# A hybrid decoder layer in emulated fp32: spread sums at the change of x, channel-major norms, and z loads placed earlier in the steps without Strassen

## The chip, the core and the metric

The kernel runs on one core of one Trainium2 chip. The metric is the device time of one execution in microseconds. Before the change it is 1374.56 us, the median of three runs (1373.44 to 1375.09).

## What is computed

One decoder layer over 2048 tokens of width 1024, all in fp32. The reference, cut to its core:

```python
def reference(x, ln_g, w_in, conv_w, lru_conv_w, ..., w_out, final_g):
    xn = rms_norm(x, ln_g)                                   # 2048 x 1024
    b_gate, c_gate, x_conv, g_conv, x_lru, g_lru = split(xn @ w_in)   # w_in: 1024 x 6144
    y_conv = b_gate * causal_conv3(c_gate * x_conv)          # 8 heads of 128 channels
    y_conv = headwise_rms_norm(y_conv, 8, conv_out_g) * silu(g_conv)
    y_lru = rg_lru_mixer(x_lru, ...)    # causal conv of width 4, two sigmoid gates per
                                        # token, scan over tokens; 16 heads of 64 channels
    y_lru = headwise_rms_norm(y_lru, 16, lru_out_g) * silu(g_lru)
    y = concatenate([y_conv, y_lru])                         # 2048 x 2048
    return rms_norm(x + y @ w_out, final_g)                  # w_out: 2048 x 1024
```

## The kernel before

**Products.** TensorE multiplies in a reduced format, so each fp32 operand is cut into a high part and a remainder. `mm` (L910) issues, for each product of blocks, sh·th, sh·tl and sl·th. The stationary side S is the weights (or z in the output projection), the moving side T is x (or w_out). Each block product of the projections is one level of a Strassen scheme: seven products per *step*, numbered 0 to 6. A product takes one *slot* of 12 matmuls of 128x512. Sums of products are formed on the way out: ScalarE copies a partial bank to `q1` after product 0 (L1220), to `u2` after product 1 (L1223) and to `rr` after product 2 (L1226), and VectorE adds these to other banks. Products 0, 1 and 2 accumulate in the same bank A, so product 1 waits for the copy to q1 and product 2 for the copy to u2.

**Steps.** The list `steps` has 48 steps of the input projection (`l`, `a`, `b` are its three kinds: the LRU group and its gate, the convolution's c and x, the convolution's b and gate), first for token half h=0 (from here on: half 0), then for half 1, and 16 steps `o` of the output projection, in two phases of eight (m = 0..7, 256 tokens each). T stays on chip as tiles `th`/`tl` within such a set of steps. There are three set changes: x of half 0 to x of half 1 (about 545 to 590 us), x to w_out for phase 0 (about 1020 to 1070 us), and the other half of w_out's rows for phase 1 (about 1195 to 1250 us).

**Set changes.** The step ahead of a change is *new*, the one behind it *opens* the set and is computed *plainly*, that is with eight block products and no Strassen, since the sums of T do not exist yet; the next is *late*. Class `Change` (L412) has a call `slot(q)` for every slot from the new step (q = 0 to 7) over the plain step (8 to 15) to the late step (16 to 21). It loads pieces of T, forms the sums (x: `sums`, four subtractions on VectorE for each of four j, at q = 9 to 12; w_out: the sums were made long before and stand in DRAM as `td`) and cuts pieces (`cut`: ScalarE casts th, VectorE subtracts to get tl). The late step takes its products in the order `AFTER` (L220) instead of `ORDER`.

**Order of the work.** Everything is under a manual schedule: program order is the order on each engine, and each engine works in that order. SP issues nearly all DMAs, also in that order, and an issue that waits for a buffer or for data holds all later ones. `at(n, f)` puts f n slots ahead; `tick()` at the head of each slot runs what is due. `load_next` (L932) loads the stationary operand for the step after next: for the input projection raw weights or cut tiles kept in DRAM (`sd`), for the output projection z. `load_z` (L269) loads y from `yd` into four `raw` pieces, the reciprocal norms from `rsd`, broadcast over partitions, into `zr`, and VectorE multiplies them (`raw<-raw,zr`). Pieces `raw` and `traw` share a pool of eight buffers, taken in turn.

**Consumers.** Each `l` step feeds `lru` (L653): a convolution, cutting u into `st` on VectorE, gate matmuls on PE (`gates`), sigmoids, a scan; `finish` (L608) multiplies the gain and the SiLU gate into `gl` (or `gb` for the convolution group), stores it to `yd`, squares y and calls `head_sums` (L598), one VectorE instruction that transposes 32x32 blocks and sums 32 tokens in each (`sums<-r`, `sums<-t`, 1024 elements per partition). After all 16 head groups of a half `head_norms` (L559) cuts the sums into `rt`, adds over channels on PE (`norm_ps`), takes the root on ScalarE and the reciprocal on VectorE (`hn`), and stores 24 pieces to `rsd` (L587). `gl`, `gb` and the residual rows `xr` take turns in two buffers of the tag `o2`. `outp` adds the residual: `xr<-xr,ob` in phase 0, `ob<-ob,xr` in phase 1, where xr comes by DMA.

The functions that the diff touches, with the line numbers of the profile:

Of the kernel before, what the change touches and what calls it, by code (L numbers as in the profile page):

```python
# [12 lines left out]
F32 = mybir.dt.float32  # L13
# [25 lines left out]
def hymba_kernel(ctx: ExitStack, tc: tile.TileContext, x, xt, w_in, par, lamc, w_gate, w_out, final_g, out):  # L39
# [14 lines left out]
    rsd = [dram.tile([2, NB, 3 * KT, P], F32, name=f"rsd{h}") for h in range(2)]  # L54
# [165 lines left out]
    AFTER = (0, 4, 5, 1, 3, 2, 6)  # L220
# [48 lines left out]
    def load_z(h, m, zr, wait):  # L269
        r = [piece("raw") for _ in range(4)]  # L270
        fs = []
        for i in range(2):
            c, b = divmod(2 * m + i, NB)
            assert normed[c // 2]
            rs_ = rsd[c // 2][c % 2]
            zz_, zq_ = [], []
            z2 = wt(("u", "r")[i], "zr") if zr else None
            for q in range(2):
                zz = r[2 * i + q].rearrange("p (k t) -> p k t", k=NB)
                zq = z2[:, q * C:(q + 1) * C] if zr else piece("zr")  # L280
                k0 = (1 - h) * KT + q * NB
                nc.sync.dma_start(zz, yd[c][b, :, k0:k0 + NB, :])
                zq = zq.rearrange("p (k t) -> p k t", k=NB)
                if h == 1:
                    nc.sync.dma_start(zq, rs_[b:b + 1, k0:k0 + NB, :].broadcast_to((P, NB, P)))
                else:
                    nc.sync.dma_start(zq[:64], rs_[b:b + 1, k0:k0 + NB, :].broadcast_to((64, NB, P)))
                    k0 += KT
                    nc.sync.dma_start(zq[64:], rs_[b:b + 1, k0:k0 + NB, :].broadcast_to((64, NB, P)))
                fs.append(lambda zz=zz, zq=zq: tt(zz, zz, zq, ALU.mult))  # L290
# [121 lines left out]
    class Change:  # L412
        def __init__(self, t, dst):
# [4 lines left out]
            self.order = [(i, j) for i in (5, 4, 0, 7, 1, 2, 3, 6) for j in range(NB)]  # L418
# [22 lines left out]
        def sums(self, j):  # L441
            b11, b12, b21, b22 = (self.r[i, j] for i in (0, 7, 4, 5))
            tt(b11, b12, b11, ALU.subtract)
            tt(b12, b22, b12, ALU.subtract)
            tt(b22, b22, b11, ALU.subtract)
            tt(b21, b21, b22, ALU.subtract)
            for i, v in ((2, b11), (3, b12), (1, b22), (6, b21)):
                self.r[i, j] = v

        def of_x(self, q):  # L450
# [11 lines left out]
            if 9 <= q <= 12:  # L462
                self.sums(q - 9)
            self.cut({1: ((5, 0), (5, 1)), 2: ((5, 2), (5, 3)), 4: ((0, 0), (0, 1)), 5: ((4, 0), (4, 1)),
# [3 lines left out]
                      18: ((6, 0),), 19: ((6, 1),), 20: ((6, 2),), 21: ((6, 3),)}.get(q, ()))  # L468
# [90 lines left out]
    def head_norms(h):  # L559
# [17 lines left out]
        def root():  # L577
            v["rs"] = aux("hn")[:NR, 0:KT * R]
            nc.scalar.activation(out=v["rs"], in_=v["ps"], func=AF.Sqrt, scale=inv_hd, bias=eps[:NR])

        def store():
            for w in range(3):
                k0 = (w + 1) % 3 * KT
                for i in range(2):
                    for b in range(NB):
                        p0 = w * R + (i * NB + b) * 4
                        nc.sync.dma_start(  # L587
                            rsd[h][i, b, k0:k0 + KT, :].rearrange("k (q r) -> q k r", q=4),
                            v["rs"][p0:p0 + 4].rearrange("q (k r) -> q k r", k=KT))
# [8 lines left out]
    def head_sums(h, kt, y):  # L598
        if summed[0] == 0:
            sums[0] = psn.tile([P, 2 * KT * R], F32, tag="sums", name="sums")  # L600
        nc.vector.tensor_reduce(out=sums[0][:, kt * R:(kt + 1) * R], in_=y.rearrange("p (a r) -> p r a", r=R),
# [6 lines left out]
    def finish(d0, h, kt, y, sil, gain):  # L608
# [10 lines left out]
        at(d0 + (1 if kt == KT and h == 0 else 2), store)  # L619
# [334 lines left out]
    with tc.manual_schedule(engines={ENG.PE, ENG.Activation, ENG.DVE, ENG.Pool, ENG.SP}):  # L954
# [182 lines left out]
        for n in range(PLAIN, N):  # L1137
# [5 lines left out]
            put = lru(h, k, 2) if opens(n) and kind == "l" else consumer[kind](h, k)  # L1143
            if n == 3 * KT + 6:
                work_on[0] = jobs()
            if opens(n):
                cc = {}
                for s, (which, i, t) in enumerate(((12, 1, 5), (22, 3, 5), (11, 1, 4), (21, 3, 4),
# [12 lines left out]
                    if s == 5:  # L1161
                        load_next(n + 2, 3)
# [123 lines left out]
```

## Time and profile before

| | |
|---|---|
| median of the runs (lowest to highest) | 1374.56 us (1373.44 to 1375.09) |
| the profiled execution's own time | 1373.37 us |
| its span | 1371.5 us |
| PE matmul busy | 1304.3 us, 95% |
| DVE (VectorE) busy | 1054.6 us, 77% |
| ACT (ScalarE) busy | 746.6 us, 54% |
| POOL (GpSimd) busy | 226.2 us, 16% |
| DMA | 355.29 MB, mean 259 GB/s |

PE's share says that the span is PE's work plus about 67 us in which it waited. In a row of a timeline the first two numbers are the start and the length in us, and a bracket at the end gives how long the engine idled just before and what released it. A group's row (page, part 5) gives busy time, mean ns of one, and the idle time before its instructions. The granted clock of TensorE is a column of its own in the table by stretches. L163 is the helper that issues every two-operand VectorE instruction and L915 the line of every projection matmul, so these rows are told apart by the names of their tiles.

### The profile page before, as it was taken

The page shows a single profiled execution, that of the slowest core. Times are in us where ns is not written, and L with a number is a line of the kernel's source. Part 1 is how long each engine was busy: PE and PEld are TensorE (multiplying, and loading weights), DVE is VectorE, ACT ScalarE, POOL GpSimd, SP SyncE. Part 2 cuts the span into 40 slices and gives each one's busy share as a digit, 9 for nine tenths or more (in the row PEclk, how much of TensorE's full clock was granted, in tenths as well). Part 3 has the DMA queues.
Part 4 walks back from the last instruction along what each step waited for, and adds up shares of the span by engine and source line. Part 5 has one row for each costly group of instructions (what it writes and reads, how often), then busy time and mean ns, then how long its engine had stood idle before and what let it go on. Part 6 is the DMA issues. An engine that isn't in the chain of part 4 may idle for free.

```text
span 1371.5 us, 16702 instructions
## 1 busy us (share of the span) xinstructions
PE 1304.3 (95%) x5648; PEld 1059.7 (77%) x5648; DVE 1054.6 (77%) x1243; ACT 746.6 (54%) x1138; POOL 226.2 (16%) x160
## 2 busy tenths in 40 slices
PE   6979999999999999898999999999999889998997
PEld 5867777787878787786888888888877678887886
DVE  6778897898989888967566785776557767659885
ACT  7475658566575667564554636364465323444443
POOL 2203333243334331101010110101100000000000
PEclk9999999999999999999999999999999999999999
DMA  7137797988989887551799999999788697797743
GB/s 282 31 127 257 279 262 264 283 318 272 344 287 321 286 289 258 172 171 50 260 318 293 330 357 317 321 361 344 232 272 282 199 253 232 244 397 270 240 149 135
DMA packets 162454, 355.29 MB, mean 259 GB/s; under 512 B 18496, under 2 KB 53312, under 8 KB 162368
## 3 DMA queue, kind: packets, MB, share of 16 engines
q1 hardware_dynamic: 162080, 353.90, 76.1%
q8 instruction: 45, 0.74, 0.2%
q14 instruction: 41, 0.34, 0.1%
q10 hardware_dynamic: 288, 0.32, 0.1%
HBM read 217.11 MB, written 137.04 MB: 258 GB/s over the span
## 4 chain that ended last, share of the span: by engine, by line
PE 39%; DMA 6%; DVE 4%; ACT 3%; issue 1%; SPq 0%; DVEq 0%; ACTq 0%
PE bank L915 38%; DMA traw<-td 3%; DMA zr<-rsd 2%; DVE tl L163 1%; PE gate L695 1%; ACT i L702 1%; ACT r L702 1%; DVE s L163 1%; DMA od<-xr 1%; DMA xr<-in_x_dram 0%; DVE raw L163 0%; ACT q L1220 0%; DVE ob L163 0%; ACT th L427 0%; DMA raw<-yd 0%
## 5 line engine op out<-in xcount | busy, mean ns | idle before, releaser
L915 PE MATMUL bank<-th,s 128*128 128x512 f32 x3632 | 1141.1, 393 | 32.7 <-ACT q L1220 15.1
L915 PEld LDWEIGHTS bank<-th,s 128*128 128x128 f32 x3632 | 686.8, 189 | 188.0 <-ACT u L1223 19.3
L915 PE MATMUL bank<-tl,s 128*128 128x512 f32 x1816 | 711.4, 392 | 1.2 <-DVE tl L163 0.9
L915 PEld LDWEIGHTS bank<-tl,s 128*128 128x128 f32 x1816 | 343.7, 189 | 74.0 <-DVE tl L163 2.5
L163 POOL TENSOR_TENSOR s<-raw,s 128x512 fp32r<-128x512 f32 x62 | 109.5, 1778 | 250.1 <-ACT s L200 209.7
L200 ACT CAST s<-raw 128x512 fp32r<-128x512 f32 x140 | 84.5, 616 | 67.6 <-PE bank L915 44.8
L163 DVE TENSOR_TENSOR tl<-traw,th 128x512 fp32r<-128x512 f32 x117 | 83.3, 747 | 40.7 <-ACT th L427 30.3
L1223 ACT COPY u<-bank 128x512 f32<-128x512 f32 x58 | 34.0, 586 | 143.2 <-PE bank L915 81.4
L163 POOL TENSOR_TENSOR gb<-gb,sg 128x1024 f32<-128x1024 f32 x16 | 40.6, 2535 | 348.0 <-ACT sg L628 288.9
L163 DVE TENSOR_TENSOR s<-s,s 128x512 fp32r<-128x512 f32 x105 | 91.5, 872 | 6.3 <-ACT s L200 6.3
L163 DVE TENSOR_TENSOR s<-raw,s 128x512 fp32r<-128x512 f32 (+1 forms) x125 | 87.8, 725 | 6.4 <-ACT s L973 4.4
L200 ACT CAST s<-s 128x512 fp32r<-128x512 f32 x105 | 64.6, 616 | 36.0 <-DVE s L163 32.7
L427 ACT CAST th<-traw 128x512 fp32r<-128x512 f32 x96 | 55.1, 617 | 34.4 <-DMA traw<-td 21.0
L1220 ACT COPY q<-bank 128x512 f32<-128x512 f32 x58 | 33.9, 584 | 70.2 <-PE bank L915 58.3
L669 DVE SCALAR_TENSOR_TENSOR u<-xl,pt,u 128x1024 f32<-128x1024 f32 x48 | 63.7, 1327 | 5.4 <-ACT u L665 4.8
L1226 ACT COPY rr<-bank 128x512 f32<-128x512 f32 x58 | 33.9, 584 | 56.5 <-PE bank L915 56.5
L163 DVE TENSOR_TENSOR raw<-raw,zr 128x512 f32<-128x512 f32 x64 | 41.9, 684 | 27.3 <-DMA zr<-rsd 27.3
L779 DVE SCALAR_TENSOR_TENSOR t<-p,pt,t 128x1024 f32<-128x1024 f32 x32 | 46.5, 1454 | 5.9 <-ACT t L776 5.1
L163 DVE TENSOR_TENSOR st<-u,st 64x1024 fp32r<-64x1024 f32 x32 | 48.7, 1521 | 1.0
L163 DVE TENSOR_TENSOR traw<-traw 128x512 f32<-128x512 f32 x60 | 44.4, 741 | 3.2 <-DMA traw<-in_w_out_dram 1.9
L702 ACT ACTIVATE r<-gate,pt 64x512 f32<-64x512 f32 x64 | 43.8, 685 | 2.2 <-PE gate L695 1.5
L702 ACT ACTIVATE i<-gate,pt 64x512 f32<-64x512 f32 x64 | 43.8, 684 | 1.1
(152 smaller groups left out, 1177.4 us busy)
## 6 DMA issues: line engine op xcount, KB each, us to landing
sd<-s SPq DMA_DIRECT2D x151, 512.0 KB
s<-sd SPq DMA_DIRECT2D x151, 512.0 KB
raw<-in_w_in_dram SPq DMA_DIRECT2D x104, 256.0 KB
raw<-yd SPq DMA_DIRECT2D x64, 256.0 KB
traw<-in_w_out_dram SPq DMA_DIRECT2D x64, 256.0 KB
so<-so SPq DMA_DIRECT2D x22, 512.0 KB
s<-so SPq DMA_DIRECT2D x22, 512.0 KB
yd<-gl SPq DMA_DIRECT2D x32, 256.0 KB
```

The lines of the kernel that those rows point to most:

```text
L163: (eng or nc.vector).tensor_tensor(out=out, in0=a, in1=b, op=op)
L200: nc.scalar.copy(dst[i][0], val(i))
L427: nc.scalar.copy(self.dst[i, j][0], self.r[i, j])
L669: nc.vector.scalar_tensor_tensor(out=v["u"], in0=o1[:, 1 + j:1 + j + N2], scalar=lw[j], in1=v["u"], op0=ALU.mult, op1=ALU.add)
L695: nc.tensor.matmul(ps[j], v["gw"][n][:, j, :], v["st"][j][:, sl], start=(n == 0), stop=(n == 1))
L702: nc.scalar.activation(out=g_[hi, sl], in_=v["ps"][j][src], func=AF.Sigmoid, bias=pt[src, bias + k:bias + k + 1])
L779: nc.vector.scalar_tensor_tensor(out=tcur["t"], in0=p[:, 2 + j:2 + j + N2], scalar=cw[j], in1=tcur["t"], op0=ALU.mult, op1=ALU.add)
L915: nc.tensor.matmul(bank, a[:, js], b, start=start and n == 0, stop=stop and n == 2, skip_group_check=more)
L1220: nc.scalar.copy(q1, bk["A"])
L1223: nc.scalar.copy(u2, bk["A"])
L1226: nc.scalar.copy(rr, bk["A"])
```

## The change

1. **Norms by channel.** `rsd` is laid out by channel instead of by token block. `head_sums` sums 32 neighbouring tokens (contiguous in a row) instead of 32 tokens with a stride of 32 elements; `head_norms` gets one more VectorE instruction, a transpose of 32x32 blocks of `norm_ps` (96x256) into `hn` ahead of the root; three stores of 32x8x32 elements take the place of 24 of 4x8x32, once per half. A z load reads a channel's 128 norms as one segment of 512 bytes where it read four channels in one segment of 2 KB, so `64x512` becomes `64x4x128` and `128x512` becomes `128x4x128`.
2. **x change.** The 16 subtractions are spread over q = 9 to 17, at most two to four in a slot, ordered by the product that needs them (`sum` for `sums`); the cuts from q = 11 on move by one or two slots; product 3 stands before product 1 in `AFTER` for all three late steps and in `Change.order`. The plain `l` step's `lru` gets one slot of delay instead of two, so its cut, gates, scan and `gl` are one slot sooner.
3. **Stores of y.** In half 1 too the first head group's `gl` (kt = 8) is stored one slot after it is made, not two.
4. **Loads in the plain step.** The plain step calls `load_next(n + 2, 4)` at its slot 3 instead of `load_next(n + 2, 3)` at slot 5. For the two plain steps of the output projection these are the z loads of m=2; their multiplications land one slot sooner.

The diff, cut to its core:

```diff
-    rsd = [dram.tile([2, NB, 3 * KT, P], F32, name=f"rsd{h}") for h in range(2)]
+    rsd = [dram.tile([1, 3 * KT, 2 * C], F32, name=f"rsd{h}") for h in range(2)]
...
-    AFTER = (0, 4, 5, 1, 3, 2, 6)
+    AFTER = (0, 4, 5, 3, 1, 2, 6)
...
-            rs_ = rsd[c // 2][c % 2]
+            rs_ = rsd[c // 2][:, :, (c % 2 * NB + b) * P:(c % 2 * NB + b + 1) * P]
...
-                    nc.sync.dma_start(zq, rs_[b:b + 1, k0:k0 + NB, :].broadcast_to((P, NB, P)))
+                    nc.sync.dma_start(zq, rs_[:, k0:k0 + NB, :].broadcast_to((P, NB, P)))
...
-            self.order = [(i, j) for i in (5, 4, 0, 7, 1, 2, 3, 6) for j in range(NB)]
+            self.order = [(i, j) for i in (5, 4, 0, 7, 3, 1, 2, 6) for j in range(NB)]
...
-        def sums(self, j):
-            b11, b12, b21, b22 = (self.r[i, j] for i in (0, 7, 4, 5))
-            tt(b11, b12, b11, ALU.subtract)
-            tt(b12, b22, b12, ALU.subtract)
-            tt(b22, b22, b11, ALU.subtract)
-            tt(b21, b21, b22, ALU.subtract)
-            for i, v in ((2, b11), (3, b12), (1, b22), (6, b21)):
-                self.r[i, j] = v
+        def sum(self, i, j):
+            b11, b12, b21, b22 = (self.r[n, j] for n in (0, 7, 4, 5))
+            a, b, dst = {2: (b12, b11, b11), 3: (b22, b12, b12), 1: (b22, b11, b22), 6: (b21, b22, b21)}[i]
+            tt(dst, a, b, ALU.subtract)
+            self.r[i, j] = dst
...
-            if 9 <= q <= 12:
-                self.sums(q - 9)
+            for i, j in {9: ((2, 0), (3, 0)), 10: ((2, 1), (3, 1)), 11: ((2, 2), (3, 2)), 12: ((2, 3), (3, 3)),
+                         13: ((1, 0), (1, 1)), 14: ((1, 2), (1, 3)), 16: ((6, 0), (6, 1)),
+                         17: ((6, 2), (6, 3))}.get(q, ()):
+                self.sum(i, j)
...
-                      11: ((1, 0),), 12: ((1, 1),), 13: ((1, 2), (1, 3)), 14: ((3, 0), (3, 1)),
-                      15: ((3, 2), (3, 3)), 16: ((2, 0), (2, 1)), 17: ((2, 2), (2, 3)),
-                      18: ((6, 0),), 19: ((6, 1),), 20: ((6, 2),), 21: ((6, 3),)}.get(q, ()))
+                      13: ((3, 0), (3, 1)), 14: ((3, 2), (3, 3)), 15: ((1, 0), (1, 1)), 16: ((1, 2), (1, 3)),
+                      17: ((2, 0), (2, 1)), 18: ((2, 2), (2, 3)), 19: ((6, 0),), 20: ((6, 1),),
+                      21: ((6, 2), (6, 3))}.get(q, ()))
...
-            nc.scalar.activation(out=v["rs"], in_=v["ps"], func=AF.Sqrt, scale=inv_hd, bias=eps[:NR])
+            nc.vector.transpose(v["rs"], v["ps"])
+            nc.scalar.activation(out=v["rs"], in_=v["rs"], func=AF.Sqrt, scale=inv_hd, bias=eps[:NR])
...
-                for i in range(2):
-                    for b in range(NB):
-                        p0 = w * R + (i * NB + b) * 4
-                        nc.sync.dma_start(
-                            rsd[h][i, b, k0:k0 + KT, :].rearrange("k (q r) -> q k r", q=4),
-                            v["rs"][p0:p0 + 4].rearrange("q (k r) -> q k r", k=KT))
+                nc.sync.dma_start(rsd[h][0, k0:k0 + KT, :].rearrange("k (p r) -> p k r", r=R),
+                                  v["rs"][w * R:(w + 1) * R].rearrange("p (k r) -> p k r", k=KT))
...
-        nc.vector.tensor_reduce(out=sums[0][:, kt * R:(kt + 1) * R], in_=y.rearrange("p (a r) -> p r a", r=R),
+        nc.vector.tensor_reduce(out=sums[0][:, kt * R:(kt + 1) * R], in_=y.rearrange("p (r a) -> p r a", a=R),
...
-        at(d0 + (1 if kt == KT and h == 0 else 2), store)
+        at(d0 + (1 if kt == KT else 2), store)
...
-            put = lru(h, k, 2) if opens(n) and kind == "l" else consumer[kind](h, k)
+            put = lru(h, k, 1) if opens(n) and kind == "l" else consumer[kind](h, k)
...
-                    if s == 5:
-                        load_next(n + 2, 3)
+                    if s == 3:
+                        load_next(n + 2, 4)
```

What this does to the order of the instructions, at three places. The first is VectorE at the x change, from the multiplication of the gain into the first half's last `gl` on. The traw tiles are the pieces of x; numbers tell the tiles apart; four rows in place on the same j are one `sums`. Before:

```order
L610 SCALAR_TENSOR_TENSOR gl_4100<-r_4429,pt_164,gl_4100 128x1024
L163 TENSOR_TENSOR traw_4439<-traw_4439 128x512
L163 TENSOR_TENSOR traw_4439<-traw_4360,traw_4439 128x512
L163 TENSOR_TENSOR traw_4360<-traw_4360,traw_4439 128x512
L163 TENSOR_TENSOR traw_4534<-traw_4534,traw_4360 128x512
L163 TENSOR_TENSOR tl_4704<-traw_4542,th_4703 128x512
L163 TENSOR_TENSOR tl_4707<-traw_4545,th_4706 128x512
L163 TENSOR_TENSOR traw_4442<-traw_4442 128x512
L163 TENSOR_TENSOR traw_4442<-traw_4362,traw_4442 128x512
L163 TENSOR_TENSOR traw_4362<-traw_4362,traw_4442 128x512
L163 TENSOR_TENSOR traw_4536<-traw_4536,traw_4362 128x512
```

And with the change:

```order
L606 SCALAR_TENSOR_TENSOR gl_4100<-r_4429,pt_164,gl_4100 128x1024
L163 TENSOR_TENSOR traw_4439<-traw_4439 128x512
L163 TENSOR_TENSOR traw_4439<-traw_4360,traw_4439 128x512
L163 TENSOR_TENSOR tl_4702<-traw_4542,th_4701 128x512
L163 TENSOR_TENSOR tl_4705<-traw_4545,th_4704 128x512
L163 TENSOR_TENSOR traw_4442<-traw_4442 128x512
L163 TENSOR_TENSOR traw_4442<-traw_4362,traw_4442 128x512
L163 TENSOR_TENSOR traw_4542<-traw_4542 128x512
L163 TENSOR_TENSOR traw_4542<-traw_4364,traw_4542 128x512
L597 TENSOR_REDUCE sums_1146<-r_4429 128x32
```

Two subtractions of each j went from here to later slots; the two cuts (tl) and what follows them stand two to six rows sooner. The 16 subtractions all still stand ahead of the two rows `st<-u,st` on which the gate matmuls wait: these are preceded by 39 instructions from that `gl` on before, and by 37 with the change.

The second place is SP behind the norms of half 0, about 604 to 617 us before. `hn` is the tile of reciprocal norms, `bd` a gate weight. Before:

```order
L587 DMA rsd0_88<-hn_5161 4x8x32 x24
L226 DMA s_5244<-sd3_97 128x1024
L304 DMA raw_5269<-in_w_in_dram 128x512
L304 DMA raw_5271<-in_w_in_dram 128x512
L304 DMA raw_5270<-in_w_in_dram 128x512
L304 DMA raw_5272<-in_w_in_dram 128x512
L615 DMA yd2_86<-gl_4669 128x4x128
L615 DMA yd3_87<-gl_4669 128x4x128
```

And with the change:

```order
L584 DMA rsd0_88<-hn_5163 32x8x32 x3
L226 DMA s_5225<-sd3_97 128x1024
L611 DMA yd2_86<-gl_4669 128x4x128
L611 DMA yd3_87<-gl_4669 128x4x128
L304 DMA raw_5251<-in_w_in_dram 128x512
L304 DMA raw_5253<-in_w_in_dram 128x512
```

The store of `gl` has 4 issues of SP between itself and the reciprocals instead of 29.

The third place is SP in the plain step that opens phase 0 of the output projection, about 1043 to 1063 us before. Before (of the twelve z loads the first six are shown):

```order
L226 DMA s_8642<-so01_119 128x1024
L838 DMA xr_8657<-in_x_dram 128x1024
L484 DMA traw_8668<-td20_126 128x512
L484 DMA traw_8670<-td21_127 128x512
L226 DMA s_8672<-so01_119 128x1024
L838 DMA xr_8688<-in_x_dram 128x1024
L484 DMA traw_8698<-td22_128 128x512
L484 DMA traw_8700<-td23_129 128x512
L282 DMA raw_8715<-yd1_85 128x512
L287 DMA zr_8719<-rsd0_88 64x512
L289 DMA zr_8719<-rsd0_88 64x512
```

And with the change (the last six z loads are shown):

```order
L282 DMA raw_8639<-yd1_85 128x512
L287 DMA zr_8648<-rsd0_88 64x4x128
L289 DMA zr_8648<-rsd0_88 64x4x128
L282 DMA raw_8640<-yd1_85 128x512
L287 DMA zr_8648<-rsd0_88 64x4x128
L289 DMA zr_8648<-rsd0_88 64x4x128
L834 DMA xr_8655<-in_x_dram 128x1024
L483 DMA traw_8666<-td20_126 128x512
L483 DMA traw_8668<-td21_127 128x512
L226 DMA s_8670<-so01_119 128x1024
L834 DMA xr_8686<-in_x_dram 128x1024
```

All twelve z loads now stand ahead of both residual loads xr and of the last four pieces of w_out; in the plain step of phase 1 the same holds for eight z loads. On VectorE the addition of the first xr still stands ahead of the four z multiplications.

More of the change, by code (lines that the diff above doesn't have):

```diff
@@ L284, in load_z @@
                 if h == 1:
-                    nc.sync.dma_start(zq, rs_[b:b + 1, k0:k0 + NB, :].broadcast_to((P, NB, P)))
+                    nc.sync.dma_start(zq, rs_[:, k0:k0 + NB, :].broadcast_to((P, NB, P)))
                 else:
-                    nc.sync.dma_start(zq[:64], rs_[b:b + 1, k0:k0 + NB, :].broadcast_to((64, NB, P)))
+                    nc.sync.dma_start(zq[:64], rs_[:, k0:k0 + NB, :].broadcast_to((64, NB, P)))
                     k0 += KT
-                    nc.sync.dma_start(zq[64:], rs_[b:b + 1, k0:k0 + NB, :].broadcast_to((64, NB, P)))
+                    nc.sync.dma_start(zq[64:], rs_[:, k0:k0 + NB, :].broadcast_to((64, NB, P)))
                 fs.append(lambda zz=zz, zq=zq: tt(zz, zz, zq, ALU.mult))
```

## The prediction

> **What bounds the kernel now.** I read the page's busy times first, then the waits, then PE's timeline wherever the table by stretches shows PE short of full.
>
> ```profile
> PE 1304.3 (95%) x5648; PEld 1059.7 (77%) x5648; DVE 1054.6 (77%) x1243; ACT 746.6 (54%) x1138; POOL 226.2 (16%) x160
> DVE raw L163 <- DMA zr<-rsd: 27.3, 13, 8.2
> 560.00:580.00 20.00, 16.24 (x61) 12.77 (x60) 19.90 (x23) 15.00 (x25) 4.38 (x3) 0.83 0.60 193
> 580.00:600.00 20.00, 20.00 (x90) 16.26 (x89) 11.29 (x14) 13.44 (x18) 0.00 (x0) 1.00 0.65 227
> 620.00:640.00 20.00, 16.67 (x70) 12.52 (x68) 18.50 (x19) 9.56 (x15) 3.92 (x3) 1.00 0.13 39
> 1060.00:1080.00 20.00, 14.43 (x53) 10.95 (x53) 12.58 (x20) 6.72 (x12) 0.00 (x0) 0.83 1.01 291
> 1100.00:1120.00 20.00, 15.85 (x60) 12.51 (x59) 13.95 (x21) 5.08 (x9) 0.00 (x0) 0.83 0.93 256
> 1200.00:1220.00 20.00, 20.00 (x90) 16.57 (x89) 10.79 (x15) 8.14 (x14) 0.00 (x0) 1.00 1.04 405
> 1240.00:1260.00 20.00, 17.98 (x71) 14.35 (x72) 16.94 (x27) 9.49 (x18) 0.00 (x0) 0.91 0.82 269
> ```
>
> The stretches give busy time (and count) of PE, its weight loads, VectorE, ScalarE and GpSimd, then the granted clock, the DMA share and GB/s. PE is full for most of the span; about 67 us of 1371.5 are its gaps. The change adds no matmul and removes none, so it acts only through gaps. Those that it touches lie at the x change (A, 560 to 580), behind the norms of half 0 (B, 620 to 645), at the first w_out change (C, 1055 to 1110) and at the second (D, 1241). PE's timeline there:
>
> ```profile
> 548.85 0.50 PE L915 MATMUL bank<-tl,s 128*128 128x512 f32 x1 [0.69 <-DVE tl L163]
> 567.63 0.79 PE L915 MATMUL bank<-th,s 128*128 128x512 f32 x1 [3.76 <-ACT q L1220]
> 626.82 0.50 PE L915 MATMUL bank<-th,s 128*128 128x512 f32 x1 [1.68 <-ACT q L1220]
> 633.94 0.50 PE L915 MATMUL bank<-th,s 128*128 128x512 f32 x1 [1.36 <-ACT u L1223]
> 640.27 0.50 PE L915 MATMUL bank<-th,s 128*128 128x512 f32 x1 [0.55 <-ACT rr L1226]
> 1059.75 0.50 PE L915 MATMUL bank<-th,s 128*128 128x512 f32 x1 [2.22 <-ACT q L1220]
> 1070.70 0.79 PE L915 MATMUL bank<-th,s 128*128 128x512 f32 x1 [1.56 <-ACT u L1223]
> 1107.36 0.79 PE L915 MATMUL bank<-th,s 128*128 128x512 f32 x1 [4.15 <-ACT q L1220]
> 1241.53 0.50 PE L915 MATMUL bank<-th,s 128*128 128x512 f32 x1 [3.57 <-ACT u L1223]
> ```
>
> A long gap costs twice. In the stretches with gaps of 3.76 and 4.15 the granted clock is 0.83 against 1.00 beside them: 3.4 us of 20, part of it in the gap itself; the first matmuls behind these gaps show 0.79 where others show 0.50. I estimate 2.5 us of slower matmuls behind each.
>
> **The change, part by part.** *A, the x change.* VectorE is busy 19.90 of 20 us there, and PE's 3.76 us is for a copy to q1 that waited behind casts, which waited for VectorE. The rows that order it:
>
> ```profile
> 578.48 2.47 DVE L163 TENSOR_TENSOR st<-u,st 64x1024 fp32r<-64x1024 f32 x2
> 581.30 0.40 PE L695 MATMUL gate<-st,bh 128*128 128x512 f32 x1
> 587.91 0.40 PE L695 MATMUL gate<-st,bh 128*128 128x512 f32 x1
> ```
>
> With the change 37 VectorE instructions stand ahead of st where 39 stood: two cuts less, 1.3 us at the 0.68 to 0.69 of 512 elements in the rows below, and I grant nearly as much again from waits for casts, so st ends at 580.95 - 2.5 = 578.5. The 16 subtractions are only moved. Product 3 ahead of product 1 gives the copy to q1 one slot more (12 matmuls; 2.72 us at full clock), so the gaps 0.69 and 3.76 and 2.5 of slow clock can go, 6.95 us at most. But the gates now stand one slot sooner on PE: PE would be at the first at 581.30 - 6.95 - 2.72 = 571.6 and must wait for st until 578.6. From there it has the slot that stood ahead of the gates before, 2.72, and what stood between the first and second gates, 587.91 - 581.30 = 6.61: the second gates come at 587.9 as before. VectorE sets this end, not PE. I take 0, with bounds of -6.95 (nothing new waits) and +2.5 (the wait for st comes in one piece, with a slow clock behind).
>
> *B, the store of gl.*
>
> ```profile
> 603.99 8.38 SPq L587 DMA_DIRECT2D rsd<-hn  x24
> 614.80 0.93 SPq L615 DMA_DIRECT2D yd<-gl  x2
> 610.32 1.28 DVE L610 SCALAR_TENSOR_TENSOR gl<-r,pt,gl 128x1024 f32<-128x1024 f32 x1
> 621.38 0.69 DVE L163 TENSOR_TENSOR gl<-bank,rr 128x512 f32<-128x512 f32 x1 [6.75 <-DMA yd<-gl]
> L595 DVE RECIPROCAL hn<-hn 96x256 f32<-96x256 f32 x2 | 3.5, 1744 | 0.0
> ```
>
> VectorE waits 6.75 us until gl is stored, since the next gl takes its buffer. 24 stores hold SP for 8.38 us, 0.35 each; three hold it for about 1.05, and the four loads of w_in step behind. So SP is ready at about 606, and what holds the store next is gl itself: it was made at 611.6 and comes one slot sooner, 608.9. From issue to VectorE the store took 6.6 us (614.80 to 621.38); issued at 609 to 609.5 it is through by 616 at the latest, where VectorE came to wait at 621.38 - 6.75 = 614.6. At most 1.4 us of the stall stay, and the gaps 1.68, 1.36 and 0.55 on PE, which lie behind this stall, go: 3.6. I take -3.6, bounds -3.6 and -2. A store of 32x8x32 has eight times the pieces of 128 bytes of one of 4x8x32; it may run longer than 0.35, which the 3 us between 606 and 609 cover. The added transpose of 96x256 stands between the matmuls and the root: as little as 0.3 us (half of the 0.68 to 0.69 of 512 elements), as much as the reciprocal of that shape, 1.74; here VectorE has 8.7 idle us in 580 to 600, and at C it lengthens the path to the norm store.
>
> *C, the first change to w_out.* Two effects against each other.
>
> ```profile
> raw<-yd SPq DMA_DIRECT2D x64, 256.0 KB
> 1045.89 0.38 SPq L838 DMA_DIRECT2D xr<-in_x_dram  x1
> 1052.58 1.22 DVE L163 TENSOR_TENSOR xr<-xr,ob 128x1024 f32<-128x1024 f32 x1 [3.26 <-DMA xr<-in_x_dram]
> 1061.26 0.69 DVE L163 TENSOR_TENSOR raw<-raw,zr 128x512 f32<-128x512 f32 x1 [3.11 <-DMA zr<-rsd]
> 1059.11 0.58 ACT L1220 COPY q<-bank 128x512 f32<-128x512 f32 x1
> 1070.06 0.58 ACT L1223 COPY u<-bank 128x512 f32<-128x512 f32 x1
> 1079.89 0.50 PE L915 MATMUL bank<-th,s 128*128 128x512 f32 x1 [1.42 <-DVE ob L163]
> ```
>
> The loss: twelve z loads (4 x 256 KB of y and as much of norms, 2.1 MB) move ahead of both xr and of four pieces of w_out. DMA is full here (share 1.01), and at the stretch's 291 GB/s 2.1 MB take 7 us, so xr, on its way from 1045.89 to 1052.58, is added at about 1059.5. VectorE adds it ahead of the z multiplications and of a pair of cuts; the last two pieces of w_out take the buffers that these cuts free, so they issue near 1061.5 and, at the 6.7 us of xr or somewhat less, land near 1066. Their casts stand ahead of the copy to q1, which comes at 1066 to 1067 instead of 1059.11. The new order of products wins one slot of 2.72, so product 1 is some 4.5 us later, with slow clock behind the gap where the old one had its slow clock at 1070.70. By then z is there: the 3.11 us for it fall away, and the copy to u2 comes at about 1074 to 1075 instead of 1070.06. Product 2 now stands right behind product 1 and shows PE the hand-over (0.64 from the copy's start to the matmul); that lies within. The 1.42 at 1079.89, which VectorE's work sets, takes up as much. I take +3.0, bounds 0 (the DMA engines had room) and +7 (nothing absorbed, a second slow clock).
>
> The gain:
>
> ```profile
> 1086.70 8.41 SPq L587 DMA_DIRECT2D rsd<-hn  x24
> 1102.32 0.69 DVE L163 TENSOR_TENSOR raw<-raw,zr 128x512 f32<-128x512 f32 x1 [8.16 <-DMA zr<-rsd]
> ```
>
> Loads of z of m=4 stand behind 24 stores; VectorE waits 8.16 us for them, then a cast, the copy to q1, and PE its 4.15 us at 1107.36. Three stores save 7.3 us and the transpose takes back at most 1.7; what is left is more than 4.15, so that gap goes with its 2.5 of slow clock, -6.6, and as PE's next gap is at 1241.53, nothing takes it back. Bounds -6.6 and -4. C together: -3.6.
>
> *D, the second change to w_out.* The same exchange of loads, without norms to store.
>
> ```profile
> 1225.21 1.23 DVE L163 TENSOR_TENSOR ob<-ob,xr 128x1024 f32<-128x1024 f32 x1 [2.62 <-DMA xr<-od]
> 1231.91 0.69 DVE L163 TENSOR_TENSOR raw<-raw,zr 128x512 f32<-128x512 f32 x1 [3.07 <-DMA zr<-rsd]
> 1240.90 0.58 ACT L1223 COPY u<-bank 128x512 f32<-128x512 f32 x1
> ```
>
> 2.1 MB at the 405 GB/s of 1200 to 1220 take 5.2 us, so xr is added at 1230.4; the chain on VectorE from there to the copy to u2 saves the 3.07 us for z and may wait 1 us for the second xr: u2 comes 2 to 3 us after 1240.90, and PE's 3.57 is a wait for just this copy. I take +2.6, bounds -3 (z was what VectorE lacked) and +6.
>
> A page of the Trainium skill bears on C and D: DMA: Bandwidth & Descriptors, section Queues, rings and completion order, says that each DMA engine consumes descriptors in ring order. It speaks against the exchange; without it xr would keep its 1052.58 and +3.0 and +2.6 would be 0. The trace holds no two orders of the same loads, so it neither shows nor denies this; what bears on it is xr's 6.7 us under way at a share of 1.01.
>
> *Half 0 and 1: the sums over tokens.*
>
> ```profile
> L601 DVE TRANSPOSE_TENSOR_REDUCE sums<-t 128x32 f32<-128x1024 f32 x16 | 33.6, 2098 | 0.0
> L695 PE MATMUL gate<-st,bh 128*128 128x512 f32 x64 | 28.2, 441 | 12.6 <-ACT hp L784 5.5 <-DVE st L163 3.7 <-ACT i L702 3.2
> ```
>
> The reduce keeps its 1024 elements, and its own row is the nearest, so 2.1 us each stays and I take 0. Were it as fast as an addition of 1024 elements (1.22), 32 instructions would get 0.88 us shorter; the gates' 3.7 us of waits for st would lose some 2.4, and A, where two lie ahead of st, another 1.5. Bounds 0 and -3.9.
>
> *Smaller.* Norm loads come in four 512-byte segments per partition instead of one of 2 KB: more packets on full DMA engines in C and D, +0.3, bounds 0 and +1.5. The store one slot sooner in half 1 is part of B.
>
> Sum: 0 - 3.6 - 3.6 + 2.6 + 0 + 0.3 = -4.3. The profiled execution took 1373.37 us (span 1371.5), 1.19 below the median; -4.3 gives 1369.1 for it and **1370.3 us** for the median.
>
> **The rivals.** *The reduce gets faster* by its contiguous view: the forecast less 3.9, 1366.4. For: 2.098 us is 1.7 times an elementwise instruction of that length. Against: the 32x32 transposition may be what costs, and no contiguous one is in this trace. The Trainium skill, Advanced Engine Details and Errata, section Memory Cachelines, states a penalty when each access hits another 16-byte line, as the old stride of 128 bytes does; no row here shows the other case.
>
> *z sooner simply helps.* The DMA engines share among loads, and xr is late by less than z is early: +3.0 at C becomes 0, +2.6 at D becomes -3: 1370.3 - 3.0 - 5.6 = 1361.7. For: VectorE waits 27.3 us for zr in all. Against: a DMA share of 0.93 to 1.04 around both places, and xr, which VectorE needs first.
>
> *The exchanged loads decide* (slower). xr is more than 10 us late, because SP holds its issue until the z loads have found buffers and full DMA engines then deliver z first; each place opens a gap of 7 us or more ahead of product 1 with slow clock behind, +7 at C and +6 at D, the segments at +1.5 and A at +2.5, for the same reason of a late feed: 2.5 - 3.6 - 6.6 + 7 + 6 + 1.5 = +6.8, 1381.4. It decides from xr some 10 us late on; at 8.5 us the loss and the gains are about equal. For: share 1.01. Against: 2.1 MB at the rates shown are 5 to 7 us.
>
> *The x change opens up.* A brings its 6.95: 1363.3. Against: gates one slot sooner with VectorE at 19.90 of 20.
>
> **How the numbers follow.** The forecast gets 0.42 (its own range 1367 to 1374), the faster reduce 0.22, z helps 0.10, the x change 0.08, the exchanged loads 0.18. This measurement tells 0.2%, 2.75 us, from no change: faster is below 1371.8, slower above 1377.3. Faster: 0.28 of the forecast's chance, 0.20, 0.10 and 0.08, 0.66; slower: 0.12 of the exchanged loads' and 0.02 of the rest, 0.14; same 0.20. The range 1361 to 1377 takes in z helps and the beginning of the exchanged loads and leaves out a little under 0.2.
>
> **What would show it.** B: no idle above 2 us before gl<-bank,rr near 615 to 621. C: the wait at 1102 gone, PE whole at 1107 with granted clock 1.00; xr added near 1059 and a larger gap before product 1. D: xr added 5 us later against the step, u2 2 to 3 us. The reduce's mean in its group's row. A: gates waiting for st by several us. Wrong if xr is not later, if the reduce is near 1.2 us, or if PE's gaps at the x change vanish without a new one at the gates.

## The result, and the profile after

The changed kernel takes 1417.1 us (median of 6 runs, 1413.87 to 1420.52) against 1375.71 us of the kernel before beside it: a ratio of 1.0298, 95% interval 1.0277 to 1.0319, slower by some 41 us where 4 us faster was forecast. The profiled execution has a span of 1416.6 us.

Of the changed kernel: from its page the busy times, the packets and one group; from the groups of VectorE the reduce and the transpose; and two rows of the table of waits (total, times, longest):

```profile
PE 1316.8 (93%) x5648; PEld 1068.0 (75%) x5648; DVE 1031.3 (73%) x1245; ACT 747.3 (53%) x1138; POOL 227.9 (16%) x160
DMA packets 186933, 355.28 MB, mean 251 GB/s; under 512 B 18400, under 2 KB 85984, under 8 KB 186848
...
L163 DVE TENSOR_TENSOR raw<-raw,zr 128x512 f32<-128x512 f32 x64 | 42.5, 684 | 48.0 <-DMA zr<-rsd 45.5 <-issue 2.4
```

```profile
L597 DVE TRANSPOSE_TENSOR_REDUCE sums<-t 128x32 f32<-128x1024 f32 x16 | 20.0, 1249 | 0.0
L578 DVE STREAM_TRANSPOSE hn<-norm_ps 96x256 f32<-96x256 f32 x2 | 0.9, 437 | 0.0
```

```profile
DVE raw L163 <- DMA zr<-rsd: 45.5, 22, 4.3
DVE xr L163 <- DMA xr<-in_x_dram: 17.3, 3, 16.8
```

The reduce fell from 2.1 to 1.25 us; the waits for z grew from 27.3 to 45.5 us, and a new wait for xr has a longest piece of 16.8. PE's timeline of the changed kernel, some of its long gaps from the x change on:

```profile
572.56 0.50 PE L911 MATMUL bank<-tl,s 128*128 128x512 f32 x1 [2.50 <-DVE tl L163]
578.82 0.80 PE L911 MATMUL bank<-th,s 128*128 128x512 f32 x1 [4.83 <-ACT u L1219]
764.23 0.79 PE L911 MATMUL bank<-th,s 128*128 128x512 f32 x1 [6.67 <-DMA s<-sd]
920.53 0.47 PE L911 MATMUL bank<-th,s 128*128 128x512 f32 x1 [2.59 <-DMA s<-sd]
1090.76 0.79 PE L911 MATMUL bank<-th,s 128*128 128x512 f32 x1 [11.42 <-ACT q L1216]
1271.34 0.80 PE L911 MATMUL bank<-th,s 128*128 128x512 f32 x1 [8.94 <-ACT q L1216]
1288.25 0.79 PE L911 MATMUL bank<-th,s 128*128 128x512 f32 x1 [3.58 <-DVE ob L163]
1301.35 0.80 PE L911 MATMUL bank<-th,s 128*128 128x512 f32 x1 [3.29 <-ACT u L1219]
```

Behind them stand VectorE's two waits for the residual rows, the first at the first change to w_out, the second at the other:

```profile
1084.35 1.23 DVE L163 TENSOR_TENSOR xr<-xr,ob 128x1024 f32<-128x1024 f32 x1 [16.79 <-DMA xr<-in_x_dram]
...
1264.79 1.23 DVE L163 TENSOR_TENSOR ob<-ob,xr 128x1024 f32<-128x1024 f32 x1 [14.24 <-DMA xr<-od]
```

Where the 45 us of span went is read by following the same matmul, the n-th of the 5648, through the profiles. The table gives, for stretches named by their times in the kernel before, by how much the start of the last matmul of the stretch moved against that of the first (this is worked out from the starts of the matmuls in the traces; f1, x1 and g1 are experiments below):

| stretch of the kernel before | changed | f1 | x1 | g1 |
|---|---|---|---|---|
| to 539 (half 0) | +2.9 | -0.4 | -0.7 | -2.5 |
| 539 to 591 (A, the x change) | +3.1 | +1.9 | +1.9 | -0.8 |
| 591 to 662 (B, store of gl) | -6.0 | -6.0 | -6.0 | -6.0 |
| 662 to 948 (half 1; z of the first four steps) | +19.1 | 0.0 | +2.0 | +1.3 |
| 1048 to 1122 (C, first change to w_out) | +6.2 | -3.3 | -5.7 | -6.0 |
| 1122 to 1231 | +1.9 | 0.0 | 0.0 | 0.0 |
| 1231 to 1270 (D, second change to w_out) | +18.3 | +3.5 | +1.7 | +0.7 |
| sum (948 to 1048 and the rest: 0) | +45.4 | -4.2 | -6.7 | -13.4 |

Half 0 runs the same instructions in the same order in every kernel that has the new reduce, and its profiles still differ by up to 7 us (+2.9 in the changed kernel, -4.2 in e4), 1.6 of them in one step near 134 us; that stretch proves nothing here.

The largest loss lies where the prediction did not look, 662 to 948: half 1's steps, in which the z of four later steps is loaded and prepared on the side. Nothing was exchanged there. Besides the shorter reduce, the only thing that the change did there is to read the norms in four pieces of 512 bytes, 4 KB apart, instead of one of 2 KB. Two of PE's gaps there, 6.67 and 2.59 us, are waits for weights (`s<-sd`); SP issues those of the first right behind z loads.

### The profile page after: what moved, and what is told of

Read it like the earlier page. It is cut to its first block, busy times and chain, and to the rows that moved or that the text cites. A ratio compares the mean times of both kernels' runs of the same rounds, so it can differ in the third digit from the quotient of the medians.

```text
span 1416.6 us, 16656 instructions
## 1 busy us (share of the span) xinstructions
PE 1316.8 (93%) x5648; PEld 1068.0 (75%) x5648; DVE 1031.3 (73%) x1245; ACT 747.3 (53%) x1138; POOL 227.9 (16%) x160
## 4 chain that ended last, share of the span: by engine, by line
PE 37%; DMA 20%; DVE 18%; ACT 7%; issue 6%; SPq 4%; POOL 0%; DVEq 0%; ACTq 0%; POOLq 0%
PE bank L911 36%; DVE s L163 4%; DMA zr<-rsd 4%; DMA traw<-td 3%; DMA raw<-yd 2%; DMA s<-sd 2%; DMA sd<-s 2%; DVE tl L163 2%; DMA raw<-in_w_in_dram 2%; ACT i L698 2%; ACT r L698 1%; PE gate L691 1%; DVE u L665 1%; DVE sums L597 1%; DMA xr<-in_x_dram 1%
## 5 line engine op out<-in xcount | busy, mean ns | idle before, releaser
L163 DVE TENSOR_TENSOR s<-s,s 128x512 fp32r<-128x512 f32 x105 | 97.0, 924 | 11.6 <-ACT s L200 11.6
L163 DVE TENSOR_TENSOR s<-raw,s 128x512 fp32r<-128x512 f32 (+1 forms) x125 | 92.6, 764 | 6.5 <-ACT s L969 4.4
L200 ACT CAST s<-s 128x512 fp32r<-128x512 f32 x105 | 64.7, 616 | 26.2 <-DVE s L163 17.6
L163 DVE TENSOR_TENSOR raw<-raw,zr 128x512 f32<-128x512 f32 x64 | 42.5, 684 | 48.0 <-DMA zr<-rsd 45.5
L163 POOL TENSOR_TENSOR gl<-gl,sg 128x1024 f32<-128x1024 f32 x16 | 40.8, 2548 | 21.0 <-ACT sg L624 20.9
```

The lines of the kernel that those rows point to most:

```text
L163: (eng or nc.vector).tensor_tensor(out=out, in0=a, in1=b, op=op)
L200: nc.scalar.copy(dst[i][0], val(i))
```

## The experiments

Ratios are of runs to runs of the kernel before on the same chip, with 95% intervals.

**Pieces or place: e1 to e4.** Two theories: P, the 512-byte pieces slow every z load; X, z ahead of xr makes the loss at the changes to w_out. e1 undoes the pieces in the changed kernel, e2 the place, e3 both; e4 is the kernel before with the norm part of the change alone.

```diff
 e1 (and e3)
-    rsd = [dram.tile([1, 3 * KT, 2 * C], F32, name=f"rsd{h}") for h in range(2)]
+    rsd = [dram.tile([2, NB, 3 * KT, P], F32, name=f"rsd{h}") for h in range(2)]
...
 e2 (and e3)
-                    if s == 3:
-                        load_next(n + 2, 4)
+                    if s == 5:
+                        load_next(n + 2, 3)
```

> The changed kernel with the norms laid out by token block again, so that a z load reads 2 KB pieces and the norms go out in 24 stores; the contiguous reduce, the transpose, the place of the z loads and the x change stay. Theory P (the 512-byte pieces slow every z load): the 19 us lost between 690 and 930 us go, and of the 24 us at the two changes to w_out only the loss by the exchanged loads stays, 3 to 6 us: 1378 us (1370 to 1385). Theory X (z ahead of xr makes the loss at the changes to w_out by itself): 1417 - 19 = 1398 us, xr still added 14 to 17 us late.

Measured: 1373.3 us, ratio 1.0002 (0.9987 to 1.0016). As P says; 44 us are in the layout of the norms, less what the 24 stores, which come back with it, cost.

> The changed kernel with the z loads of the plain steps back at slot 5, behind xr and the pieces of w_out; the 512-byte pieces stay. Theory P: the 19 us between 690 and 930 stay, and z is late at both changes to w_out, though xr is not: 1403 us (1395 to 1412). Theory X: the 24 us at the changes to w_out go: 1392 us (1388 to 1395).

Measured: 1399.26 us, ratio 1.0186 (1.0156 to 1.0216). As P says.

> Both undone: 2 KB pieces with 24 stores, z loads back at slot 5; the contiguous reduce with its transpose, the x change, the earlier store of gl stay. Both theories: 1370 us (1364 to 1375): the shorter reduce and the earlier store of gl gain up to 6, the x change costs up to 3, the gap behind the 24 stores at 1107 stays.

Measured: 1371.65 us, ratio 0.9986 (0.9969 to 1.0002). Against e1 the place costs about 2 us when pieces are 2 KB, with intervals that overlap; e2 against the changed kernel it costs 15 when they are short. Most of X's harm needs P's.

> The kernel before with the first part of the change alone: contiguous reduce, transpose, norms by channel in three stores, 512-byte pieces. Theory P: slower, some 19 us between 690 and 930 and 5 to 10 at the changes to w_out, against 4 to 10 gained by the stores and the reduce: 1392 us (1385 to 1402). Theory X: faster, since nothing is exchanged: 1367 us (1362 to 1371).

Measured: 1394.03 us, ratio 1.0158 (1.012 to 1.0195). P again: without any exchanged load, +17.6 us between 662 and 948 and +11.4 at D by the matmuls' starts, against gains of -0.8 at A and -6.0 at B.

What an exchanged load does with 2 KB pieces shows in e1's timelines, of SP (the first and the last of the twelve z loads and xr behind them) and then of VectorE, ScalarE and PE:

```profile
1041.67 0.38 SPq L282 DMA_DIRECT2D raw<-yd  x1
...
1050.14 0.44 SPq L289 DMA_DIRECT2D zr<-rsd  x1
1050.78 0.44 SPq L838 DMA_DIRECT2D xr<-in_x_dram  x1
...
1056.64 1.23 DVE L163 TENSOR_TENSOR xr<-xr,ob 128x1024 f32<-128x1024 f32 x1 [12.08 <-DMA xr<-in_x_dram]
...
1063.45 0.58 ACT L1220 COPY q<-bank 128x512 f32<-128x512 f32 x1
...
1064.09 0.80 PE L915 MATMUL bank<-th,s 128*128 128x512 f32 x1 [7.75 <-ACT q L1220]
...
1105.10 0.50 PE L915 MATMUL bank<-th,s 128*128 128x512 f32 x1 [4.09 <-ACT q L1220]
```

xr is late, the copy to q1 is late behind the casts, and PE waits 7.75 us ahead of product 1. xr is late because SP comes to it late: against the matmuls beside it, which start 3.9 us sooner here than in the kernel before, it is issued 8.8 us later (1050.78 against 1045.89), and from its issue to the addition it takes 5.9 us where it took 6.7. The last row is the gap behind the 24 stores, which e1 has again.

**What is wrong with the pieces: e7, e9, f4, g3.** Three theories: M1, a piece costs its time whatever it holds; M2, the broadcast is slow, since 64 or 128 partitions ask the same place for each piece; M3, the 4 KB between the pieces are what is wrong. e7 gives the kernel before as many 512-byte pieces, in y, where no two partitions read the same bytes; e9 is e4 with one number changed.

```diff
 e7
-    yd = [dram.tile([NB, P, 2 * KT, P], F32, name=f"yd{c}") for c in range(NC)]
+    yd = [dram.tile([NB, 2 * KT, P, P], F32, name=f"yd{c}") for c in range(NC)]
...
 e9 (f4: R, 128 bytes, for P; g3: 2 * C, 4 KB)
-    rsd = [dram.tile([1, 3 * KT, 2 * C], F32, name=f"rsd{h}") for h in range(2)]
+    rsd = [dram.tile([1, 3 * KT, 2 * C + P], F32, name=f"rsd{h}") for h in range(2)]
```

> The kernel before with only y laid out by channel, so that a z load reads y in four pieces of 512 bytes per partition and the norms in 2 KB pieces; the number of 512-byte pieces in a z load is that of the changed kernel, but no two partitions read the same bytes. Theory M1 (a piece costs its time whatever it holds): as slow as the norms in such pieces, 1395 us (1388 to 1402). Theory M2 (the broadcast is what is slow: 64 or 128 partitions ask the same place for each piece): 1376 us (1373 to 1380).

Measured: 1373.2 us, ratio 0.9993 (0.9979 to 1.0007). M1 falls: as many short pieces cost nothing.

> The kernel before with the first part of the change alone, as run before, and 512 bytes of padding behind each channel's norms, so that the four pieces of a load lie 4.5 KB apart instead of 4 KB. Theory M3 (a stride of 4 KB sends the four pieces to one place of the memory): back to 1360 us (1355 to 1370). M1 and M2: unchanged, 1394 us (1389 to 1399).

Measured: 1358.51 us, ratio 0.9875 (0.9856 to 0.9894). M3: 36 us, 1394 to 1358, are the distance between the pieces.

The packets of e7, of e4 and of e9, a row of each page: their numbers are within 100 of each other.

```profile
DMA packets 187030, 355.29 MB, mean 259 GB/s; under 512 B 18496, under 2 KB 86080, under 8 KB 186944
```

```profile
DMA packets 186933, 355.28 MB, mean 256 GB/s; under 512 B 18400, under 2 KB 85984, under 8 KB 186848
```

```profile
DMA packets 186933, 355.28 MB, mean 262 GB/s; under 512 B 18400, under 2 KB 85984, under 8 KB 186848
```

The first z load of half 1 in the table by stretches, e4 (its loads are issued from 652.76 on) and then e9 (from 654.16 on). The last three columns are granted clock, DMA share and GB/s:

```profile
656.00:658.00 2.00, 2.00 (x10) 1.68 (x9) 1.97 (x2) 0.21 (x1) 0.00 (x0) 1.00 0.57 151
658.00:660.00 2.00, 2.00 (x10) 1.65 (x10) 1.28 (x1) 0.38 (x1) 0.00 (x0) 1.00 0.63 179
660.00:662.00 2.00, 2.00 (x11) 1.65 (x10) 1.49 (x2) 0.00 (x0) 0.00 (x0) 1.00 0.68 183
```

```profile
656.00:658.00 2.00, 2.00 (x10) 1.65 (x10) 1.83 (x3) 0.54 (x2) 0.00 (x0) 1.00 0.92 247
658.00:660.00 2.00, 2.00 (x11) 1.65 (x10) 1.97 (x2) 0.59 (x1) 0.00 (x0) 1.00 1.01 241
660.00:662.00 2.00, 2.00 (x11) 1.65 (x10) 0.77 (x2) 0.00 (x0) 0.00 (x0) 1.00 1.17 201
```

In e4 the DMA engines are not full in these six us in which the loads are under way: 0.57 to 0.68 against 0.92 and more. In the two us ahead of them, at the start of the loads, it is the other way round, 0.90 in e4 and 0.60 in e9.

> e9 with 128 bytes of padding instead of 512. If it is enough that the pieces do not lie at a multiple of 4 KB from each other: 1358 us, as e9. If a distance of a piece's own length or more is needed: between 1362 and 1394 us.

Measured: 1365.69 us, ratio 0.9946 (0.9928 to 0.9963). Most of the loss goes with 128 bytes; 7 us of it (against g1) to 10 us (against e9) stay. Whether these come of the distance between the pieces or of where the pieces start, no run tells.

> e9 with 4 KB of padding instead of 512 bytes, so that the pieces of a load lie 8 KB apart. If pieces a multiple of 4 KB apart are served one after the other: 1394 us, as e4 (1388 to 1400). If it was that one distance: 1358 us.

Measured: 1568.15 us, ratio 1.142 (1.1392 to 1.1448). Both guesses missed: 8 KB apart is neither harmless nor as bad as 4 KB, it is six times as bad (210 us against 36 over e9). The row of DMA issues gives the median from issue to landing, here of the 128 KB and 256 KB norm loads in the changed kernel, in e9 and in g3:

```profile
zr<-rsd SPq DMA_DIRECT2D x64, 128.0 KB, 7.2
...
zr<-rsd SPq DMA_DIRECT2D x32, 256.0 KB, 8.9
```

```profile
zr<-rsd SPq DMA_DIRECT2D x64, 128.0 KB, 5.8
...
zr<-rsd SPq DMA_DIRECT2D x32, 256.0 KB, 6.5
```

```profile
zr<-rsd SPq DMA_DIRECT2D x64, 128.0 KB, 12.3
...
zr<-rsd SPq DMA_DIRECT2D x32, 256.0 KB, 15.3
```

Distance alone is not it either: e7's pieces lie 64 KB apart, at no cost. What is slow in these runs is the two together, many partitions asking for the same few pieces, and these at 4 or 8 KB from each other; pieces at 4 or 8 KB that each partition reads for itself were not run. Why the two together are slow stays open.

**The norm part in a layout without the fault: e5.** Norms are kept by groups of four channels and blocks of 32 tokens, so that three stores remain and a load reads 2 KB in one piece; VectorE takes the norms in another order in its multiplication.

```diff
+    rsd = [dram.tile([6, R, 4 * R], F32, name=f"rsd{h}") for h in range(2)]
...
+                zq = zq.rearrange("p (q k r) -> p k q r", q=4, k=NB)
+                zz = zz.rearrange("p k (q r) -> p k q r", q=4)
```

> The kernel before with the contiguous reduce and the transpose, and norms laid out by groups of four channels and 32 tokens: three stores as in the change, and z loads in 2 KB pieces as before (VectorE reads the norms back in the order channel, block, token). No x change, no exchanged place. If the 512-byte pieces were all that was wrong with the first part of the change, its gains stay whole: -4 to the x change by the shorter reduce, -6 behind the norms of half 0, -6 at 1107: 1358 us (1354 to 1363). If fewer and larger stores or the reduce cost something at the w_out change: 1365 or more.

Measured: 1359.97 us, ratio 0.9885 (0.9864 to 0.9905). The gains of the norm part are whole.

> e9 again (the kernel before with the norm part, 512 bytes of padding), beside the next three: ratio 0.9875 as before, 1358 us.

Measured: 1359.45 us, ratio 0.9894 (0.9876 to 0.9912).

> The kernel before with the contiguous reduce and the transpose alone; 24 stores and 2 KB pieces as before. The reduce is 0.85 us shorter 32 times (1.25 against 2.1), the waits for st shrink by 1.3 us in half 0 and the x change by 1.5: 1371 us (1369 to 1373), so that the three stores are worth the remaining 11 us. If the reduce is worth more: 1366 us.

g4 is the kernel before with the reduce and the transpose alone (two lines).

Measured: 1368.4 us, ratio 0.9964 (0.995 to 0.9979): the reduce is worth some 5 us, between the two guesses, and the three stores about 9.5, by g1 beside it. The stalls that the stores removed, in e9's timeline of VectorE, where the kernel before has 6.75 and 8.16 us:

```profile
611.88 0.69 DVE L163 TENSOR_TENSOR gl<-bank,rr 128x512 f32<-128x512 f32 x1 [0.81 <-DMA yd<-gl]
...
1086.90 0.69 DVE L163 TENSOR_TENSOR raw<-raw,zr 128x512 f32<-128x512 f32 x1 [0.90 <-DMA zr<-rsd]
```

**The rest of the change on top: f1, x1, f2, f3, g2.** f1 is the whole changed kernel with the 512 bytes of padding.

> The whole changed kernel, with one number other: 512 bytes of padding behind each channel's norms. If the 4 KB between the pieces is the cause of all that went wrong: x1 plus what the exchanged place costs, 1362.5 + 1.7 (by e1 against e3) = 1364 us (1361 to 1368). If the exchanged place does harm of its own with short pieces: 1372 us or more.

Measured: 1367.27 us, ratio 0.9961 (0.9947 to 0.9975). Faster than before, by about what the prediction said of the whole change, and slower than its norm part alone. It lies at the upper end of the first expectation, 1361 to 1368. In the table its C and D together are 4 us behind those of x1, which has the z loads in their old place (by the ratios the two are 8 us apart): with quick pieces the exchange costs 2 us (e1 against e3) to 4 us or more.

> The changed kernel with the norms laid out as in e5 (three stores, 2 KB pieces) and the z loads back at slot 5: the x change and the earlier store of gl are what it has beyond e5. By the profiles of e3 and e4 the x change costs 2 to 3 us: e5 plus 2.5, about 1361 us. If it gains what it was made for: 1352 us.

Measured: 1362.48 us, ratio 0.9904 (0.9887 to 0.9922): 2.5 us above e5 beside it, with intervals that overlap. x1's timeline of ScalarE and of PE at the x change:

```profile
568.99 0.50 PE L913 MATMUL bank<-tl,s 128*128 128x512 f32 x1 [2.49 <-DVE tl L163]
...
571.38 2.10 ACT L678 CAST st<-u 64x1024 fp32r<-64x1024 f32 x2 [10.01 <-DVE tl L163]
...
574.63 0.58 ACT L1221 COPY u<-bank 128x512 f32<-128x512 f32 x1
...
575.26 0.79 PE L913 MATMUL bank<-th,s 128*128 128x512 f32 x1 [4.83 <-ACT u L1221]
```

The gap for q1 is gone. In its place stand one of 2.49 us for a cut of VectorE's and one for u2 of 4.83 us, and the granted clock between 570 and 580 is 0.66: ScalarE waits ahead of its cast to st, by the row for VectorE's cuts, and the copy to u2 is behind it.

f2 is e9 with only the order of products of the change (`AFTER` and `Change.order`), f3 is x1's change with padding and the gates two slots late, g2 is f3 with the old order of products.

> e9 (the kernel before with the norm part, padded) with only the order of the products changed: 3 ahead of 1 in the three late steps, and in the order of the pieces of w_out. Theory O (product 2 right behind product 1 shows PE the copy to u2, and the slot won for q1 is worth less): +1 to +3 at the x change and the two changes to w_out together, 1361 us. Theory S (the order is harmless, the sooner gates do the harm): 1358 us or less.

Measured: 1364.34 us, ratio 0.9936 (0.9921 to 0.995), against 0.9875 and 0.9894 of e9 and g1 on other chips: the order alone costs 6 to 8 us, more than theory O asked for. PE's two gaps at the changes to w_out in f2, then those in e9:

```profile
1069.47 0.79 PE L912 MATMUL bank<-th,s 128*128 128x512 f32 x1 [3.73 <-ACT u L1220]
...
1233.95 0.80 PE L912 MATMUL bank<-th,s 128*128 128x512 f32 x1 [5.19 <-ACT u L1220]
```

```profile
1061.66 0.79 PE L912 MATMUL bank<-th,s 128*128 128x512 f32 x1 [1.91 <-ACT u L1220]
...
1226.76 0.80 PE L912 MATMUL bank<-th,s 128*128 128x512 f32 x1 [3.68 <-ACT u L1220]
```

The copy to u2 is the late one at both places, and product 3 no longer runs in front of it. Over the whole stretches this costs nothing: by the matmuls' starts C and D are -7.9 and +0.8 in f2, -7.3 and +0.9 in e9. The loss is at the x change, +3.5 in f2 against -0.9 in e9. PE's gaps there, f2's and then e9's:

```profile
566.79 0.50 PE L912 MATMUL bank<-tl,s 128*128 128x512 f32 x1 [1.70 <-DVE tl L163]
...
576.30 0.80 PE L912 MATMUL bank<-th,s 128*128 128x512 f32 x1 [3.32 <-ACT u L1220]
```

```profile
564.09 0.80 PE L912 MATMUL bank<-th,s 128*128 128x512 f32 x1 [2.92 <-ACT q L1217]
```

> e9 with the whole x change and the earlier store of gl, but the plain l step's lru delayed by two slots as before instead of one; z loads at slot 5. In x1 ScalarE waited 10 us in its cast to st, for VectorE's cuts, with the casts and the copy to u2 behind it. Theory S: with the gates later that wait stands behind those casts, the gap of 4.8 us goes, 1355 us (1352 to 1358). Theory O: 1362 us, as x1.

Measured: 1362.22 us, ratio 0.9924 (0.9912 to 0.9937), as theory O has it; later gates take the u2 gap from 4.83 to 3.16 and no further. Theory S is not out by this, since in f3 too ScalarE waits (3.00 us) ahead of its cast to st, and the copy to u2 stands behind that cast.

> f3 with the order of products of before: spread sums, the cuts of 3 ahead of those of 1, the earlier store of gl, gates two slots late, padding. Theory O (the order of products makes the loss): 1357 us or less, the sums spread gain a little at the x change. Theory S' (the spread sums make it): 1362 us as f3.

Measured: 1361.36 us, ratio 0.9904 (0.9883 to 0.9924), beside g1's 0.9894: the spread sums neither gain nor lose what these runs can tell. f3 against g2 puts some 3 us on the order of products, with intervals that overlap, less than f2 against e9; between 3 and 8 us its size stays open. By the matmuls' starts the x change is +1.5 in f3 and +0.2 in g2.

So e9 (or e5) beats both kernels: 1358.5 to 1360 us, 1.1 to 1.25% below the kernel before.

## Why the prediction was wrong, point by point

- **The step that failed is "Smaller".** It priced the four short segments at +0.3 with bounds 0 and 1.5, by counting packets on the DMA engines. The same change with 512 bytes of padding is at 0.9961, without it at 1.0298: the term is 46 us (0.0337 of 1374.56). More packets there are, 24479 in all, but they are beside the point: about as many in e7 and as many in e9 cost nothing. The trace of before held norm loads of 2 KB pieces alone, and nothing of pieces that lie apart. A changed stride in memory was an operation that no row covered, and its bound should have stayed open above. It also fell on the z of four steps that is loaded in half 1 (+19.1 between 662 and 948), which the prediction left out; it priced the segments in C and D alone.
- **With that term taken out, the sum held.** f1's regions against the prediction's: C -3.3 (forecast -3.6), D +3.5 (+2.6), A +1.9 (0, bound +2.5), B -6.0 (-3.6, bound -3.6: too little, since gaps of PE too small to be quoted went too, and with every gap the longer matmuls behind it), in all -4.2 in the profile against -4.3. That the total fits is in part luck: the errors of A and B nearly cancel, and the reduce, put at nothing, is in it with a gain. B's two causes were not both needed: e9, without the sooner gl, has -6.0, and e1, with 24 stores, -5.9.
- **The exchanged loads.** From xr on the chain was as told, and its sizes are seen in e1: xr added at 1056.64 with a wait of 12.08 us, 9 us more than before, PE waiting 7.75 us for q1. Its first link was another: the prediction let xr wait 7 us on the DMA engines, behind 2.1 MB, but xr is issued 8.8 us later and is no slower under way (5.9 us against 6.7). That the sizes agree is luck. The rival "the exchanged loads decide" had the late issue and the right places, 16.79 and 14.24 us of wait for xr and gaps of 11.42 and 8.94 ahead of product 1; but its cause, order alone, is false: with quick pieces the place costs 2 us (e1 against e3) to 4 us (f1 against x1 in the table).
- **The rule of ring order** in the Trainium skill (DMA: Bandwidth & Descriptors, Queues, rings and completion order) spoke against the exchange. No run here shows it at work: in e1 xr comes late by its issue, not by its time under way.
- **The reduce.** Taken at 2.1, measured at 1.25 us: the rival was right, worth 5 us (g4) where 3.9 was worked out. The Trainium skill's page (Advanced Engine Details and Errata, Memory Cachelines) speaks of a penalty when each access hits another line; the rows agree, 2.10 against 1.25 for the same 1024 elements.
- **The transpose** took 0.44 us, near the lower bound of 0.3.
- **The x change** was forecast at 0, because VectorE and not PE sets its end. PE's gap of 3.76 for q1 did go, and gaps of 2.50 for a cut and 4.83 for u2 came, as new waits: +1.9 in f1, +3.1 in the changed kernel. The prediction looked for them at the gates; they came earlier, at VectorE's cuts and at the copy to u2 behind the cast that feeds the gates. That VectorE sets the end is borne out by e9 and g1, which are one kernel: between 560 and 570 the granted clock is 0.66 in e9 and 1.00 in g1, g1 has two gaps of PE more (1.54 and 0.53), and the stretch comes out alike, -0.9 and -0.8. So the prediction's "a long gap costs twice" does not hold where PE would have to wait anyway.
- **Product 2 right behind product 1** was folded into C as harmless, and at the changes to w_out it is (f2 against e9). At the x change, where the prediction did not look for it, the new order of products costs 1.3 us (f3 against g2) to 4.4 us (f2 against e9) by the matmuls' starts, and 3 to 8 us by the runs.

## What to carry to other kernels

When an edit moves data in memory, price its distances as well as its pieces: how many readers ask for the same bytes, and how far apart the next bytes are that they ask for. A broadcast load whose pieces lie 4 or 8 KB apart is worth one run with a little padding before anything else is explained. Where a load comes late, look first at when it was issued. And where a change has several parts, follow the same matmul through both traces first: the stretch in which nothing was meant to change is the one that names the cause.

## What the runs showed of the hardware

- Broadcast loads of four 512-byte pieces run as fast at 4.5 KB apart as one piece of 2 KB (1358.5 us in e9, 1360.0 in e5), slower at 4 KB (a norm load 7.2 instead of 5.8 us from issue to landing, some 36 us in the kernel) and far slower at 8 KB (12.3 us, some 210 us in the kernel). 128 bytes off the 4 KB recover most (1365.7 us in f4). Pieces of that size that every partition reads for itself, 64 KB apart, cost nothing (1373.2 us in e7).
- In six us in which the 4 KB loads of e4 are under way the DMA engines show a share of 0.57 to 0.68, at the same place in e9 0.92 to 1.17: a load can be slow though its engines are not full.
- Twelve loads ahead of a thirteenth on SP made it 8.8 us later at its issue and no slower behind it (5.9 us to its use against 6.7; e1 and the kernel before).
- The transposing reduce of 1024 elements takes 1.25 us on neighbours and 2.10 us at a stride of 128 bytes.
